# A causal depthwise convolution in two half-rate sums taken by turns, planned transfers, and filler products in TensorE's planned pauses

## The chip, the cores and the metric

One core of a Trainium2 chip runs the whole program. The metric is the time of one execution in device microseconds (us); lower is better. The kernel before took 1378.37 us as the median of three runs (1372.61 to 1379.06). PE is TensorE (products), PEld its weight loads, DVE is VectorE, ACT is ScalarE, POOL is GpSimd, SP is the engine that issues most transfers.

## The reference

One inference step of a two-layer streaming encoder: 512 prompt frames and 64 frames of a running stream, 1024 features. Each layer, cut to what matters:

```
proj = x @ w_in                       # columns q, k, v, conv_a, conv_gate
k, q = rope(k), rope(q)
attn = differential attention, 4 heads (softmax of q k, two maps subtracted, times v)
u    = conv_a * sigmoid(conv_gate)
c    = causal depthwise conv of u, 31 taps, 512 channels, + conv_b
c    = silu(layer_norm(c))
y    = concat(attn, c) @ w_out
x    = layer_norm(alpha * x + y)
x    = layer_norm(alpha * x + relu(x @ w_ff1)^2 @ w_ff2)
```

Outputs are y of both streams and the new k, v and convolution states of both layers.

## The kernel before, in words

All 576 frames are handled at once, features on partitions, in two groups of 288 frames. Products are made in three passes (`tri`, lines 733 to 736): every operand is split into a high and a low part, and high·high, high·low and low·high are summed in one PSUM bank. A layer reads 92 weight units of 128 x 1024 numbers. `weights` (line 830) loads a unit into a `raw` buffer from SP's queue (L861); ScalarE makes the high part `wh` (L891), and the low part `wl` is made in one of two ways: VectorE or GpSimd subtracts (L894), or ScalarE writes minus raw (L875) and a transfer on GpSimd's queue adds the unit from DRAM onto it (L878, "by_dma"); how often the second is used is set by the knob `DM`. Twenty units of layer 1 are split ahead of time during layer 0 (`split_ahead`, L815 and L819).

A layer has five parts: projections with attention and convolution woven into them; the output projection with residuals (L1799, L1804, L1857); a layer norm (`layer_norm`: sums of the residuals L1835, means L1029 and L1034, subtractions L1052, squares L1058 and their adds L1064, variance by products with a column of ones L1006, scale L1133 and L1141, and the split into the next operands L1154); the feed-forward part; and a second layer norm.

The convolution (`conv`, line 1305) is done for each of four tiles of 128 channels over 606 positions (30 of history, 512, 30 of history, 64, with the positions between the streams computed and dropped). Of its 31 taps, the first `NPTS[t]` are products on ScalarE (L1319 with the bias, L1322) that GpSimd adds up (L1325); the others are a chain on VectorE, each a multiply-add into one accumulator in PSUM that waits for the one before it (L1335 and L1337). A closing (L1344, three instructions) adds the two sums and drops the unused positions. Only one tile at a time may hold the VectorE chain (`cv`).

The order of all work is written by a planner in the kernel (`Sched.run`, line 565), before anything runs: every operation is a node with its engines, planned costs (`cV`, `cA`, `cG`, `cP`, `cD`), dependencies, buffers and a priority, and an event loop gives each engine the ready node of the highest priority. A node with several engines goes where it would end first. Priorities and choices come from tables of knobs (`PHASES`), one for each of the eight phases. On the chip every engine keeps its planned order, and waits for what it needs.

Of the kernel before, what the change touches and what calls it, by code (L numbers as in the profile page):

```python
# [16 lines left out]
D = 1024  # L17
# [12 lines left out]
UC = UB - HIST  # L30
S0 = SEQ + HIST
# [54 lines left out]
def cP(n, passes=1):  # L86
# [50 lines left out]
PD = 0.1  # L137
DM, GD, GDL = 0.0, 0.88, 6.5
PRP, PRS = 889.2, -10.4
# [12 lines left out]
PHASES = [{'CH': 4,  # L152
# [3 lines left out]
  'KA': 4,  # L156
  'KB': 8,
  'KR': 4,
  'LD1': 1.46,
  'LD2': 3.53,  # L160
  'LD3': -0.78,
  'LDO': -373.3,
  'LP': 2.08,
  'LPE': 2.98,
  'LPT': 2.46,
  'NPT': '9,9,9,10',
  'PA': 158.2,
# [12 lines left out]
  'QL0': '0 2 4 6',  # L180
  'QL1': '0 2 4 5 6 7',
  'QLF': '0 6 7',
  'RG': 1,
  'RP': [0, 2],
  'RS': 1,
  'S2F': [0, 1, 2, 3, 5],
  'S2H': [0, 2, 4, 7],
  'SHP': 1,
  'SQ': 'k0 q0 g0 a0 v0 g1 a1 q1 g2 a2 k1 v1 g3 a3 q2 k2 v2 q3 k3 v3',
  'VP': 0.39,  # L190
  'VS': 2.22,
# [2237 lines left out]
```

## Time and profile before

| | |
|---|---|
| median of three runs | 1378.37 us |
| profiled execution | 1375.67 us |
| its span, first to last instruction | 1373.9 us |
| TensorE busy | 1308.0 us, 9518 instructions |
| VectorE busy | 1078.1 us, 2206 |
| ScalarE busy | 705.1 us, 1413 |
| GpSimd busy | 302.3 us, 292 |
| mean granted clock of TensorE | 0.977 |
| layer 0: attention, convolution, output projection | about 0 to 276 us |
| layer 0: feed-forward at full pace | 375 to 675 us |
| layer 1: attention, convolution, output projection | about 705 to 950 us |
| layer 1: feed-forward at full pace | 1025 to 1350 us |

Busy time is not pace: products are pipelined, so TensorE counts as busy at half clock too. "PEclk" is the clock that was granted, 1.00 being full. A group's "idle before" is the time that its engine waited ahead of it, with what ended that wait.

### The profile page before, as it was taken

To read this page: it belongs to the slowest core of one execution; us is meant where nothing else is said; L and a number is where in the kernel's file an instruction comes from. 1 tells how busy PE (TensorE), PEld (TensorE's weight loads), DVE (VectorE), ACT (ScalarE), POOL (GpSimd) and SP (SyncE) were. 2 spreads that over 40 slices of the span, in tenths; PEclk is the share of its full clock that TensorE was granted. 3 is DMA by queue.
4 is the path that set the end of the run, shared out by engine and by line. 5 is a ranking of instruction groups with operands and counts; after the bars stand their busy time and mean duration, and the time that the engine had idled before them with its cause. 6 is when DMAs were issued, how large, how long until landed. Compare 5 with 4: busy or idle time off the path is not lost.

```text
span 1373.9 us, 24858 instructions
## 1 busy us (share of the span) xinstructions
PE 1308.0 (95%) x9518; PEld 1264.1 (92%) x9518; DVE 1078.1 (78%) x2206; ACT 705.1 (51%) x1413; POOL 302.3 (22%) x292
## 2 busy tenths in 40 slices
PE   8989989979999999999999999899989999999997
PEld 7878879979899999999998988798889999999996
DVE  5899998777888887878658999868677676767737
ACT  5766677265444444434156657754654443434424
POOL 0456620150000000000144885223400000000013
PEclk9999989989999999999999999899999999999998
DMA  6635533334465645554345444454234343435262
GB/s 220 162 94 140 122 117 106 93 130 156 144 211 165 208 168 192 185 167 139 102 158 204 160 152 121 129 135 118 64 79 117 112 108 108 124 80 144 70 152 69
DMA packets 70102, 186.38 MB, mean 136 GB/s; under 512 B 10848, under 2 KB 16608, under 8 KB 69984
## 3 DMA queue, kind: packets, MB, share of 16 engines
q1 hardware_dynamic: 63504, 161.20, 34.9%
q0 software_dynamic: 6480, 23.60, 10.4%
q8 instruction: 75, 1.23, 0.4%
q14 instruction: 43, 0.35, 0.1%
HBM read 154.11 MB, written 30.65 MB: 134 GB/s over the span
## 4 chain that ended last, share of the span: by engine, by line
PE 72%; DVE 18%; issue 3%; DMA 2%; ACT 2%; POOL 2%; SPq 0%; ACTq 0%; DVEq 0%; POOLq 0%
PE b L734 21%; PE b L735 21%; PE b L736 21%; DVE sc L1337 8%; DMA raw<-in_wu_dram 2%; PE sc L734 1%; PE b L1006 1%; POOL sq L1064 1%; PE sc L736 1%; PE b L1568 1%; PE sc L735 1%; DVE nm L1486 1%; DVE P L1530 1%; DMA wl<-in_wu_dram 1%; PE b L1611 1%
## 5 line engine op out<-in xcount | busy, mean ns | idle before, releaser
L734 PE MATMUL b<-x,wh 128*128 128x288 f32 x1356 | 416.2, 307 | 6.6 <-ACT wh L891 4.0
L736 PE MATMUL b<-x,wl 128*128 128x288 f32 x1356 | 406.1, 299 | 7.0 <-DVE wl L894 4.8
L735 PE MATMUL b<-x,wh 128*128 128x288 f32 x1356 | 406.5, 300 | 1.7 <-DVE x L1215 1.1
L734 PE MATMUL b<-a,wh 128*128 128x288 f32 x1088 | 325.0, 299 | 0.2 <-ACT x L731 0.2
L735 PE MATMUL b<-a,wh 128*128 128x288 f32 x1088 | 321.3, 295 | 0.0
L736 PE MATMUL b<-a,wl 128*128 128x288 f32 x1088 | 321.0, 295 | 0.0
L734 PEld LDWEIGHTS b<-x,wh 128*128 128x128 f32 x1356 | 260.5, 192 | 13.5 <-ACT wh L891 4.0
L736 PEld LDWEIGHTS b<-x,wl 128*128 128x128 f32 x1356 | 260.2, 192 | 8.2 <-DVE wl L894 5.3
L735 PEld LDWEIGHTS b<-x,wh 128*128 128x128 f32 x1356 | 260.6, 192 | 4.0 <-DVE x L1215 2.5
L734 PEld LDWEIGHTS b<-a,wh 128*128 128x128 f32 x1088 | 205.1, 188 | 2.0 <-issue 0.6
L735 PEld LDWEIGHTS b<-a,wh 128*128 128x128 f32 x1088 | 205.4, 189 | 0.5
L736 PEld LDWEIGHTS b<-a,wl 128*128 128x128 f32 x1088 | 205.1, 188 | 0.0
L2273 DVE TENSOR_TENSOR r<-r,b 128x288 f32<-128x288 f32 x192 | 85.7, 450 | 87.6 <-PE b L736 87.3
L1337 DVE SCALAR_TENSOR_TENSOR sc<-ub,par,sc 128x606 f32<-128x606 f32 x160 | 136.2, 851 | 4.2
L878 POOL DMA_DIRECT2D wl<-in_wu_dram x45 | 39.2, 871 | 446.8 <-ACT wl L875 387.6
L1064 POOL TENSOR_TENSOR sq<-sq,sq 128x288 f32<-128x288 f32 x40 | 35.7, 910 | 416.1 <-ACT sq L1058 415.5
L1325 POOL TENSOR_TENSOR r<-r,prod 128x606 f32<-128x606 f32 x72 | 113.7, 1580 | 54.8 <-ACT prod L1322 31.0
L891 ACT CAST wh<-raw 128x1024 fp32r<-128x1024 f32 (+1 forms) x73 | 71.4, 979 | 71.2 <-PE b L735 52.3
L2056 ACT CAST wh<-ckv 128x512 fp32r<-128x512 f32 x104 | 64.1, 620 | 76.7 <-PE b L735 61.2
L894 DVE TENSOR_TENSOR wl<-raw,wh 128x1024 fp32r<-128x1024 f32 (+1 forms) x73 | 84.5, 1161 | 22.3 <-ACT wh L891 21.7
L1884 DVE TENSOR_TENSOR wl<-ckv,wh 128x512 fp32r<-128x512 f32 x104 | 71.1, 685 | 6.0 <-ACT wh L2056 5.8
L875 ACT ACTIVATE wl<-raw 128x1024 fp32r<-128x1024 f32 x45 | 47.7, 1060 | 44.2 <-PE b L736 25.5
(320 smaller groups left out, 2409.9 us busy)
## 6 DMA issues: line engine op xcount, KB each, us to landing
raw<-in_wu_dram SPq DMA_DIRECT2D x110, 512.0 KB, 4.6
wl<-in_wu_dram POOLq DMA_DIRECT2D x45, 512.0 KB, 7.2
wscr<-cs SPq DMA_DIRECT2D x80, 256.0 KB, 2.0
ckv<-in_wu_dram SPq DMA_DIRECT2D x26, 512.0 KB, 3.6
ah<-in_wu_dram SPq DMA_DIRECT2D x26, 512.0 KB, 4.4
cs<-in_wu_dram SPq DMA_DIRECT2D x40, 256.0 KB, 2.8
wh<-wscr SPq DMA_DIRECT2D x20, 512.0 KB, 3.3
wl<-wscr SPq DMA_DIRECT2D x20, 512.0 KB, 4.4
```

The lines of the kernel that those rows point to most:

```text
L734: TE.matmul(o, wh, xh, start=start, stop=False)
L735: TE.matmul(o, wh, xl, start=False, stop=False)
L736: TE.matmul(o, wl, xh, start=False, stop=stop)
L875: S.activation(wt["lo"], wt["raw"], AF.Copy, scale=-1.0)
L891: S.copy(wt["hi"][:, c], wt["raw"][:, c])
L894: e.tensor_tensor(wt["lo"][:, c], wt["raw"][:, c], wt["hi"][:, c].bitcast(F32), op=ALU.subtract)
L1064: e.tensor_tensor(q[a]["t"], q[a]["t"], q[b]["t"], op=ALU.add)
L1325: GP.tensor_tensor(cc[t], cc[t], st[j], op=ALU.add)
L1337: V.scalar_tensor_tensor(st["a0"], win(j), w, st["a0"], op0=ALU.mult, op1=ALU.add)
L1884: e.tensor_tensor(o, a, b, op=ALU.subtract)
L2056: S.copy(tl["wh"][box["i"]][:, off:off + n], src())
L2273: V.tensor_tensor(rr, rr, bk(), op=ALU.add)
```

## The change

**The convolution.** Even and odd frames are taken apart. With e the even and o the odd frames, the 16 even taps and the 15 odd taps make three half-length sums: a = even taps on e, b = odd taps on o (with the bias), c = sums of neighbouring taps on e + o. The even outputs are a + b, the odd ones c − a − b (b one place on), corrected by the bias. b is on ScalarE and GpSimd as before (304 elements, `NPTS` of the 15 taps, what remains on VectorE); a and c are on VectorE, 16 products each of 303 elements, by turns: one of a, one of c. e + o is one addition, on VectorE or GpSimd. The summed taps (`cv`) are made once in a layer. Results lie with the even frames first; the split of the convolution's output into `cmix` puts them back in order (`halves`).

**Fillers.** When the planner's clock stands at a moment at which TensorE has nothing to do, has been busy less than `FT` = 0.6 of the last `FW` = 2 us, and a PSUM bank is free, it plans a product of constants into that bank (`keep`). There are 23 in the program: 12 ahead of the first real product, 8 at the first layer norm of layer 0 and just ahead of it, one at the second, and two at the last.

**Transfers planned.** The accumulating transfer (L878) is planned with a duration on the transfer queue and a latency behind what is queued there (`dm`, `GDL`, `GDS`), not with a fixed 6.5; some other planned costs are changed.

**The tables.** All eight tables of knobs, the split-ahead priorities and `PD` are others. So the whole order of work is another.

What the order of instructions shows for the whole program: accumulating transfers 45 → 60, VectorE's weight subtractions of 1024 elements 65 → 50 (10 → 5 ahead of the first layer norm, 38 → 19 from there to the second layer's start, 2 → 7 in layer 1 up to its first norm), ScalarE's tap products 80 → 112, GpSimd's adds of them 72 → 104, the odd taps on VectorE 0 → 8 (5 and 3). Of layer 0's residual additions of 288 (L1804), all 16 were on VectorE, and 15 are now on GpSimd; of the 12 adds of its sums (L1835), 3 were on GpSimd, and now all are. TensorE's real products are the same.

```diff
+FT, FW, FC = 0.6, 2.0, 0.23
-PD = 0.1
-DM, GD, GDL = 0.0, 0.88, 6.5
+PD = 0.0
+DM, GD, GDL, GDS = 0.0, 0.88, 1.9, 2.93
...
-PHASES = [{'CH': 4,
+PHASES = [{'CH': 3,
...
-  'NPT': '9,9,9,10',
+  'NPT': '15,10,16,15',
...
+    def spare(self, t, busy, avail):
+        if not FT or self.keep is None or busy > t + 1e-9 or not self.free["b"] or not self.left_p():
+            return False
+        return sum(min(b, t) - max(a, t - FW) for a, b in self.recent if b > t - FW) < FT * FW
...
+                        if n.dm:
+                            n.lat = GDL + n.dm + max(0.0, busy["D"] - t - c)
+                            busy["D"] = max(busy["D"], t + c) + n.dm
...
+            if self.spare(t, busy["P"], avail):
+                n = self.op({"P": FC}, lambda e: self.keep(e, self.free["b"][0]))
...
+    def keep(e, k):
+        TE.matmul(tl["b"][k][:, :128], ones_d, ones_d, start=True, stop=True)
+    sch.keep = keep
...
+            V.tensor_tensor(cv[:, :, 1:], taps[:, :, 2::2], taps[:, :, 1::2], op=ALU.add)
+            V.tensor_scalar(cv[:, :, 0], pr[:, P_CB:P_CG], 2.0, None, op0=ALU.mult)
...
-                los.append(op({"G": GD}, acc, (m,), lat=GDL, pri=pri + 1000, two=False))
+                los.append(op({"G": GD}, acc, (m,), lat=GDL + GDS, pri=pri + 1000, two=False))
+                los[-1].dm = GDS
...
         def conv(t, start, outs):
-            hc = UC // 2
-            npt = NPTS[t]
+            npt = min(NPTS[t], W // 2)
...
-                    w = pr[:, cw + j:cw + j + 1]
+                    w = pr[:, cw + 2 * j + 1:cw + 2 * j + 2]
...
-                        st[j] = take("prod")
-                        S.activation(st[j], ub[t][:, j:j + UC], AF.Copy, scale=w)
+                        st[j] = take("prod")[:, :YH + 1]
+                        S.activation(st[j], frames(1, j, YH + 1), AF.Copy, scale=w)
...
+            for j in range(npt, W // 2):
+                def vb(e, j=j):
+                    V.scalar_tensor_tensor(b_(), frames(1, j, YH + 1), pr[:, cw + 2 * j + 1:cw + 2 * j + 2], b_(),
+                                           op0=ALU.mult, op1=ALU.add)
+            def both(e):
+                e.tensor_tensor(cc[t][:, :UH], frames(0, 0, UH), frames(1, 0, UH), op=ALU.add)
...
-            for j in range(npt, W):
+            for j in range(W // 2 + 1):
...
-                        V.scalar_tensor_tensor(st["a0"], win(j), w, st["a0"], op0=ALU.mult, op1=ALU.add)
-                vt = op({"V": cV(UC, True) + 0.06}, va, (*start, pd, vt), acq=("cv", "sc") if j == npt else (), pri=PT)
+                        V.scalar_tensor_tensor(st["a"], frames(0, j, YH), w, st["a"], op0=ALU.mult, op1=ALU.add)
+                def vc(e, j=j):
+                        V.scalar_tensor_tensor(st["c"], cc[t][:, j:j + YH], w, st["c"], op0=ALU.mult, op1=ALU.add)
+                vt = a_end = op({"V": 0.45}, va, (*start, pd, vt), acq=("cv", "sc") if j == 0 else (), pri=PT)
+                vt = op({"V": 0.45}, vc, (sm, vt, ld_n), pri=PT)
...
-                    V.tensor_tensor(a1[:, o:o + n], a1[:, i:i + n], a0[:, b, c:c + n], op=ALU.add)
+                for o, i, n in parts:
+                    V.tensor_tensor(cc[t][:, o:o + n], st["a"][:, i:i + n], b_(n, i), op=ALU.add)
+                for o, i, n in parts:
+                    V.scalar_tensor_tensor(cc[t][:, T // 2 + o:T // 2 + o + n], st["c"][:, i:i + n], cv[:, t, 0:1],
+                                           b_(n, i + 1), op0=ALU.add, op1=ALU.subtract)
+                for o, i, n in parts:
+                    z = cc[t][:, T // 2 + o:T // 2 + o + n]
+                    V.tensor_tensor(z, z, st["a"][:, i:i + n], op=ALU.subtract)
```

More of the change, by code (lines that the diff above doesn't have):

```diff
@@ L407 @@
   'DM': 0.5,
+  'KA': 3,
+  'KB': 0,
+  'KR': 5,
+  'LA': 0.28,
+  'LD1': 1.28,
+  'LD2': -1.07,
+  'LD3': -0.17,
+  'LDO': 100.5,
+  'LDS': 1000,
+  'LP': 0.81,
+  'LPE': 2.12,
+  'LPT': -2.77,
+  'PA': -72.0,
+  'PC': 684.3,
+  'PCN': 1357.5,
+  'PE_': 267.8,
+  'PK': -422.4,
+  'PN': 644.4,
+  'PQ': 9.9,
+  'PR': 562.7,
+  'PS': -860.1,
+  'PT': 1313.0,
+  'PV': 430.4,
+  'PW': -719.8,
+  'PX': -183.1,
+  'QL0': '0 6',
+  'QL1': '0 6 7',
+  'QLF': '0 2 4 6 7',
+  'RG': 0,
+  'RP': [1, 4, 5],
@@ new lines @@
+  'RS': 1,
+  'S2F': [2, 3, 6],
+  'S2H': [1, 3, 4, 5],
+  'SHP': 1,
+  'VP': -0.06,
+  'VS': 1.38,
+  'WP': 0.5,
+  'WP2': -1.19,
+  'WP3': -1.59},
+ {'CH': 3,
+  'CS': 0,
+  'CSTD': 2,
+  'DM': 0.5,
+  'KA': 6,
+  'KB': 8,
+  'KR': 4,
+  'LA': 0.35,
+  'LD1': 0.84,
+  'LD2': 1.43,
+  'LD3': -0.99,
+  'LDO': -1004.4,
+  'LDS': 200,
+  'LP': 0.47,
+  'LPE': 0.86,
+  'LPT': -1.23,
+  'PA': -528.5,
+  'PC': -0.1,
+  'PCN': 1014.7,
+  'PE_': -456.9,
+  'PK': -105.2,
+  'PN': 45.5,
+  'PQ': -41.9,
+  'PR': -328.1,
+  'PS': 427.4,
+  'PT': 1173.3,
+  'PV': 351.8,
+  'PW': -1518.1,
+  'PX': 730.8,
+  'QL0': '0 6 7',
+  'QL1': '0 4 6 7',
+  'QLF': '0 2 4 6 7',
+  'RG': 0,
+  'RP': [0, 1, 2, 3, 4, 6],
+  'RS': 0,
+  'S2F': [3, 5],
+  'S2H': [0, 5, 6, 7],
+  'SHP': 0,
+  'VP': -0.41,
+  'VS': 0.91,
+  'WP': 0.24,
+  'WP2': -0.3,
+  'WP3': -2.36},
@@ new lines @@
+ {'CH': 2,
+  'CSTD': 2,
+  'DM': 0.34,
+  'KA': 1,
+  'KB': 4,
+  'KR': 3,
+  'LA': 0.6,
+  'LD1': 2.87,
+  'LD2': 1.66,
+  'LD3': 1.49,
+  'LDO': 53.6,
+  'LDS': 500,
+  'LP': -1.78,
+  'LPE': -0.59,
+  'LPT': 1.93,
+  'NPT': '14,16,16,13',
+  'PA': 700.3,
+  'PC': -92.8,
+  'PCN': 891.1,
+  'PE_': 839.8,
+  'PK': -847.6,
+  'PN': -840.6,
+  'PR': 113.9,
+  'PS': 194.6,
+  'PT': 497.7,
+  'PV': 529.6,
+  'PW': -141.6,
+  'PX': -1361.9,
+  'QL0': '0 2 4 5 6 7',
+  'QL1': '0 6 7',
+  'QLF': '0 2 4 6',
+  'RG': 0,
+  'RP': [0, 3, 7],
+  'RS': 1,
+  'S2F': [3, 6, 7],
+  'S2H': [0, 1, 2, 3],
+  'SHP': 0,
+  'SQ': 'k0 q0 g0 a0 g1 v0 q1 a1 g2 a2 k1 g3 v1 a3 q2 k2 v2 k3 q3 v3',
+  'VP': 0.43,
+  'VS': 1.36,
+  'WP': -1.48,
+  'WP2': -0.99,
+  'WP3': -1.5},
@@ new lines @@
+ {'CH': 2,
+  'CS': 1,
+  'CSTD': 2,
+  'DM': 0.34,
+  'KA': 2,
+  'KB': 3,
+  'KR': 6,
+  'LA': 0.85,
+  'LD1': 1.91,
+  'LD2': 1.13,
+  'LD3': 2.99,
+  'LDO': 3.4,
+  'LP': 0.42,
+  'LPE': 0.72,
+  'LPT': -0.26,
+  'PA': -314.7,
+  'PC': 196.8,
+  'PCN': 403.2,
+  'PE_': 610.9,
+  'PK': -901.0,
+  'PN': 1022.7,
+  'PQ': -23.5,
+  'PR': 272.9,
+  'PS': -800.1,
+  'PT': 1293.5,
+  'PV': 154.3,
+  'PW': 459.0,
+  'PX': -424.6,
+  'QL0': '0 2 4 6',
+  'QL1': '0 4 6 7',
+  'QLF': '0 4 6 7',
+  'RG': 1,
+  'RP': [1, 2, 6, 7],
+  'RS': 0,
+  'S2F': [0, 6, 7],
+  'S2H': [1, 5],
+  'SHP': 0,
+  'VP': -0.78,
+  'VS': -0.24,
+  'WP': -0.74,
+  'WP2': -0.47,
+  'WP3': 2.29},
@@ L746, in xt, with halves @@
         return take("x")
+    def halves(z):
+        return z.rearrange("p (n two) -> p two n", two=2)
     def at(dt=F32R):
@@ L1207, in x_nodes @@
         ld = chain.pop("x%d%d" % (k, g))
[L1208 removed]
+        d = op({"D": cD(200)}, ld, (xfn.get(k),), acq=("a",) if g == 0 else (), lat=DL, pri=pri)
         sl = GS[g]
```

558 lines of the change are left out of this document (217 added, 341 removed).

## The prediction

> **What bounds the kernel now.** I read the page first, then the table of busy time by stretch, then the chain of work cut to the stretches that fall short, then single lines. The page says that TensorE is the bound over the whole span, with VectorE second:
>
> ```profile
> PE 1308.0 (95%) x9518; PEld 1264.1 (92%) x9518; DVE 1078.1 (78%) x2206; ACT 705.1 (51%) x1413; POOL 302.3 (22%) x292
> ...
> PE   8989989979999999999999999899989999999997
> ...
> PEclk9999989989999999999999999899999999999998
> ```
>
> A mean of 95% hides two kinds of stage. In the table by stretch the columns are the microseconds, then busy time with its instructions for PE, PEld, DVE, ACT and POOL, then the granted clock, the DMA share and GB/s:
>
> ```profile
> 50.00:175.00 125.00, 114.33 (x804) 108.46 (x804) 118.98 (x189) 85.75 (x170) 78.55 (x61) 0.95 0.49 119
> 175.00:225.00 50.00, 46.08 (x313) 39.62 (x312) 44.96 (x111) 40.91 (x102) 9.31 (x8) 0.90 0.33 97
> 276.00:300.00 24.00, 16.47 (x83) 15.06 (x82) 16.48 (x38) 14.45 (x32) 14.59 (x16) 0.72 0.38 131
> 375.00:675.00 300.00, 300.00 (x2264) 299.84 (x2263) 241.90 (x477) 121.76 (x213) 0.00 (x0) 1.00 0.51 170
> 725.00:900.00 175.00, 164.75 (x1166) 151.43 (x1165) 161.29 (x297) 118.62 (x268) 103.33 (x81) 0.96 0.49 150
> 1025.00:1350.00 325.00, 324.94 (x2456) 324.38 (x2454) 225.75 (x469) 137.53 (x238) 18.91 (x22) 1.00 0.41 109
> ```
>
> The two feed-forward stretches (625 us) are full at clock 1.00: nothing planned elsewhere can shorten them. What TensorE can give back lies in the attention and convolution stretches. From 50 to 225 it idles 14.6 us (175 less 114.33 less 46.08) and loses about 10 us to the clock (0.05 of 114 us and 0.10 of 46 us); from 725 to 900 it idles 10.3 us and loses about 6.6; from 276 to 300 it idles 7.5 and loses about 4.6 (0.28 of 16.5 us). In the first and the third VectorE is busy 95% and 92%. The chain of waits, cut to 50–175 and to 725–900, names the work that is waited for; these are its shares by line:
>
> ```profile
> by line: DVE sc L1337 37.0%; issue 6.5%; DMA raw<-in_wu_dram 5.0%; DVE P L1530 4.2%; PE b L734 3.9%; PE b L735 3.5%; PE b L736 3.5%; DVE nm L1486 3.4%; DVE wl L894 2.7%; ACT prod L1322 1.8%; DVE rc L1518 1.8%; ACT wl L875 1.6%; DVE r L1344
> ```
> ```profile
> by line: DVE sc L1337 35.2%; issue 6.9%; PE b L734 4.8%; PE b L1568 4.0%; PE b L735 4.0%; PE b L736 3.9%; DVE P L1530 3.3%; DVE nm L1486 3.1%; DVE nm L1492 2.0%; DVE sc L1335 1.9%; DVE swp L1367 1.9%; PE b L1006 1.7%; PE sc L734 1.7%; DVE r
> ```
>
> L1337 is VectorE's tap of the convolution: 46 us of the chain in the first stretch, 62 in the other. There the softmax pieces that TensorE needs stand in VectorE's queue between taps.
>
> **The change on VectorE.** Lines of VectorE by total time, cut to 50–225 (busy us, mean ns of one, idle before), and below them the taps of 725–900:
>
> ```profile
> L1337 DVE SCALAR_TENSOR_TENSOR sc<-ub,par,sc 128x606 f32<-128x606 f32 x81 | 68.9, 851 | 1.9
> ...
> L894 DVE TENSOR_TENSOR wl<-raw,wh 128x1024 fp32r<-128x1024 f32 x5 | 7.1, 1424 | 0.0
> ...
> L1344 DVE TENSOR_TENSOR r<-r,sc 128x303 f32<-128x303 f32 (+2 forms) x12 | 3.5, 350 | 0.5 <-POOL r L1325 0.5
> ```
> ```profile
> L1337 DVE SCALAR_TENSOR_TENSOR sc<-ub,par,sc 128x606 f32<-128x606 f32 x77 | 65.6, 852 | 2.3
> ```
>
> What a tap of 303 costs no row shows, so I build it. The timeline has six taps in a row, and five subtractions that do not depend on one another; two groups give the slope:
>
> ```profile
> 119.39 5.28 DVE L1337 SCALAR_TENSOR_TENSOR sc<-ub,par,sc 128x606 f32<-128x606 f32 x6
> ```
> ```profile
> 279.91 1.91 DVE L1052 TENSOR_TENSOR r<-r,b 128x288 f32<-128x288 f32 x5
> ```
> ```profile
> L2083 DVE TENSOR_TENSOR ckh<-ah 128x512 f32<-128x512 f32 x26 | 17.8, 685 | 1.8 <-DMA ah<-in_wu_dram 1.8
> ...
> L1052 DVE TENSOR_TENSOR r<-r,b 128x288 f32<-128x288 f32 x56 | 21.7, 447 | 3.3 <-PE b L1034 3.1
> ```
>
> A tap now waits for the one before: (5.28 − 0.85) / 5 = 0.886 us from start to start, 35 ns more than its length. Independent work of 288 elements starts every (1.91 − 0.45) / 4 = 0.365 us, 82 ns less than its length. An element costs (685 − 447) / 224 = 1.06 ns, so a tap of 303 should last 851 − 322 = 530 ns. In turns, neither sum waits for its neighbour: 0.53 − 0.08 = 0.45 us a start. Should each still wait: 0.565 us.
>
> Per layer: before, layer 0 has 87 taps on VectorE (77.1 us at 0.886) and four closings (3.5 us), 80.6 in all; layer 1 has 81 and four, 75.3. After, each has 128 products of the two sums (57.6 us at 0.45), layer 0 five odd taps (2.3) and layer 1 three (1.4), two frame sums (0.8), and four closings of six instructions, three of 256 elements and three of 32. For a closing I take 1.5 us (bounds 1.1, the three long ones at 0.365, and 2.4, all six at 0.4): 6.0. Sum 66.7 and 65.8, so VectorE loses 14 us in layer 0 and 9.5 in layer 1; at 0.565 it would lose nothing (81.4 and 80.5).
>
> The Trainium skill ("VectorE: DVE Perf Modes", section "The DRAIN you can't avoid") says that an instruction of VectorE does not start before the pipe has emptied and that chaining doesn't help, so that the count of instructions should be kept low: it speaks against cutting taps in two. By the page's formula for a two-input fp32 operation, (N+151)/0.96, 303 elements would take 473 ns and the sum an estimated 3 us more per layer. The starts 0.365 us apart above are shorter than that formula's 457 ns for 288, so the trace does not bear it out for independent work.
>
> VectorE, first convolution tile of layer 0; before:
>
> ```order
> L1337 SCALAR_TENSOR_TENSOR sc_119<-ub_544,par_161,sc_119 128x2x303 x3
> L1485 MEMSET sc_118 64x2x64
> L1486 TENSOR_REDUCE nm_594<-sc_118 128x2
> L1337 SCALAR_TENSOR_TENSOR sc_119<-ub_544,par_161,sc_119 128x2x303 x7
> L1485 MEMSET sc_118 64x2x64
> ```
> and now the same place (ub is the even frames, r the frame sums):
> ```order
> L1421 SCALAR_TENSOR_TENSOR sc_118<-r_92,cv_165,sc_118 128x303
> L1414 SCALAR_TENSOR_TENSOR sc_118<-ub_548,par_161,sc_118 128x303
> L1576 MEMSET sc_119 64x2x64
> L1577 TENSOR_REDUCE nm_591<-sc_119 128x2
> L1421 SCALAR_TENSOR_TENSOR sc_118<-r_92,cv_165,sc_118 128x303
> ```
> Whole taps give way to the two sums by turns; softmax work stands between them as before, now behind shorter neighbours.
>
> How much reaches the end: of layer 0's 77 us of taps 46 lie on the chain, so 14 freed give 8. Five weight splits (L894) leave VectorE before the first layer norm, at 1.42 us each by the row above (7.1 us); the chain gives L894 2.7% of 125 us, 3.4 us, of half the splits that remain: I take 2. With about 1 for queueing: −11 in layer 0, at most −24 (the whole shortfall). In layer 1, 62 of 72 us are on the chain: 9.5 freed give 8; but five splits come to VectorE there, up to 7 us, I charge 4: −4.
>
> **What else moves.** ScalarE and GpSimd compute the odd taps, 304 elements instead of 606, 112 products instead of 80 and 104 adds instead of 72. Their rows, and those of the additions of 288 on GpSimd and on VectorE:
>
> ```profile
> L1325 POOL TENSOR_TENSOR r<-r,prod 128x606 f32<-128x606 f32 x72 | 113.7, 1580 | 54.8 <-ACT prod L1322 31.0 <-issue 20.8
> ...
> L1322 ACT ACTIVATE prod<-ub,par 128x606 f32<-128x606 f32 x72 | 56.7, 801 | 11.9 <-POOL r L1325 11.5
> ...
> L1064 POOL TENSOR_TENSOR sq<-sq,sq 128x288 f32<-128x288 f32 x40 | 35.7, 910 | 416.1 <-ACT sq L1058 415.5
> ...
> L1835 DVE TENSOR_TENSOR sg<-sg,r 128x288 f32<-128x288 f32 x34 | 16.1, 473 | 1.0
> ...
> L1804 DVE TENSOR_TENSOR r<-r,x 128x288 f32<-128x288 f32 x32 | 15.6, 491 | 0.9
> ```
>
> At about 0.95 us an addition takes 104 × 0.95 = 99 us of GpSimd instead of 114, and stays behind VectorE: nothing. Fifteen more weights get their low half by an accumulating transfer from GpSimd's queue, 17 more of them in the first feed-forward stretch, where TensorE is full: nothing. But in layer 0, 15 residual additions and 9 more of the sums' 12 ahead of the first layer norm go to GpSimd. GpSimd there, before:
>
> ```order
> L878 DMA wl_90<-in_wu_dram 128x1024
> L1064 TENSOR_TENSOR sq_102<-sq_102,sq_103 128x288
> L1064 TENSOR_TENSOR sq_104<-sq_104,sq_105 128x288
> L1064 TENSOR_TENSOR sq_106<-sq_106,sq_103 128x288
> L1064 TENSOR_TENSOR sq_102<-sq_102,sq_104 128x288
> L1064 TENSOR_TENSOR sq_102<-sq_102,sq_106 128x288
> L1835 TENSOR_TENSOR sg_108<-sg_108,r_98 128x288
> ```
> and now (sg is the sum that the mean's product reads):
> ```order
> L1896 TENSOR_TENSOR r_94<-r_94,x_2504 128x288
> L1927 TENSOR_TENSOR sg_107<-r_97,r_91 128x288
> L1927 TENSOR_TENSOR sg_107<-sg_107,r_95 128x288
> L1927 TENSOR_TENSOR sg_107<-sg_107,r_92 128x288
> L1927 TENSOR_TENSOR sg_107<-sg_107,r_96 128x288
> L1927 TENSOR_TENSOR sg_107<-sg_107,r_93 128x288
> L1927 TENSOR_TENSOR sg_107<-sg_107,r_98 128x288
> ```
> The sum is now six GpSimd links in a row, before each half's mean. TensorE's planned pause at the same place, before and now:
> ```order
> L1034 MATMUL b_115<-r_91,ones_d 128x288
> L734 MATMUL b_117<-x_2987,wh_83 128x288
> L735 MATMUL b_117<-x_2988,wh_83 128x288
> L736 MATMUL b_117<-x_2987,wl_87 128x288
> L734 MATMUL b_117<-x_3001,wh_83 128x288
> ```
> ```order
> L782 MATMUL b_116<-x_3189,wh_84 128x288
> L783 MATMUL b_116<-x_3188,wl_88 128x288
> L786 MATMUL b_114<-ones_d 128x128 x6
> L781 MATMUL b_114<-x_3130,wh_85 128x288
> L782 MATMUL b_114<-x_3131,wh_85 128x288
> ```
> Six filler products now stand where TensorE will wait for the normalised x. They can be weighed with the stall of today:
>
> ```profile
> 276.00:284.00 8.00, 2.73 (x16) 2.05 (x14) 7.98 (x21) 7.91 (x20) 6.48 (x9) 0.95 0.17 65
> 284.00:297.00 13.00, 10.75 (x46) 10.13 (x47) 6.24 (x13) 4.83 (x9) 7.51 (x7) 0.50 0.57 187
> ```
> ```profile
> 284.97 0.61 PE L736 MATMUL b<-x,wl 128*128 128x288 f32 x1 [4.83 <-DVE wl L894]
> ```
> ```profile
> L1539 PE MATMUL b<-ident,P 128*128 128x128 f32 x80 | 15.9, 300 | 7.2 <-DVE P L1530 4.3 <-DVE rc L1517 1.9 <-DVE ob L1615 0.6
> ```
>
> After 5 us of pause the clock is half for 13 us, with 10.75 busy: 5.4 us lost. The nearest row prices a filler at 0.30 us, so 23 cost 7 us if all stood on the path, and they stand in pauses. The Trainium skill ("TensorE: Matmul & The Clock Gate", Part 1) says that the clock halves after an idle window of some 3.4 us and returns after a busy one; the row at 0.50 behind the pause agrees. Gain: up to 5.4 from the clock and 4.83 from the split, which now stands ahead of the norm's subtractions; loss: 9 sums at 0.91 instead of 0.47, 4.0, and half of the 15 residuals at 0.42 more, 3. I take 0, bounds −10 and +10. Twelve fillers stand before the first real product:
>
> ```profile
> 0.00:4.00 4.00, 0.00 (x0) 0.00 (x0) 0.46 (x1) 2.12 (x3) 0.86 (x12) 1.00 0.47 123
> 4.00:10.00 6.00, 5.97 (x19) 4.87 (x20) 4.27 (x10) 4.12 (x11) 0.00 (x0) 1.00 0.87 269
> ```
>
> The first 19 products run 0.31 us apart, though they follow each other at 300/2264 = 0.133 us in the full stretch. Fillers started at 1 us at half pace (0.6 each) end near 8: they delay the start by 4 and spare up to 3.4. Zero, give or take 2.
>
> **Sum.** −11 − 4 + 0 + 0 = −15 us against the profiled execution (1375.67 us, span 1373.9), which is 2.7 under the median: 1378.4 − 15 = 1363 us.
>
> **Rivals.** (A) *Both attention stretches become bound by TensorE*: all 24 us of the first shortfall and half of the second's 17 go, and 5 of the norm: −37, 1341. For it speaks the chain; against it, that softmax, rotary and split work stay on VectorE. (B) *The halves don't pay*: each tap waits as today, 0.565 us, and conv work is equal; left are the splits, 0 to −5: 1376. Against it: nothing between neighbours depends. The Trainium skill's section on the drain, quoted above, would have it come out near this. (C) *Slower: GpSimd's sums at layer 0's norm.* They decide when GpSimd needs over about 1 us an addition, as in its row at 282.07 below; the 24 additions moved there at 1.2 instead of 0.48 end 17 us later, and the pause behind brings a half clock (5): −15 + 17 + 5 = +7, 1385.
>
> ```profile
> 282.07 7.19 POOL L1064 TENSOR_TENSOR sq<-sq,sq 128x288 f32<-128x288 f32 x6 [0.46 <-ACT sq L1058]
> ```
>
> (D) *No difference to see*: with every instruction moved, gains are given back at places I cannot see; within 7 us of 1378.
>
> **How the numbers follow.** This kernel's measurement tells about 0.5% (6.9 us) from no change. Forecast (−8 to −28): 0.50; A: 0.12; B and D: 0.20; C: 0.18. Faster 0.62, same 0.20, slower 0.18. The forecast's own range is 1350 to 1370; A below and B, D and part of C above widen it to 1342–1384, which leaves out about a tenth on either side.
>
> **What would show it.** Right: taps of 303 starting 0.45 us apart; VectorE's busy time about 25 us lower before the first norm; TensorE's idle and half clock between 50 and 225 down from 24 us to about 13; feed-forward stretches of 300 and 325 us as now; no clock of 0.50 at the first norm. Wrong: taps 0.565 apart (B), TensorE waiting on sg from GpSimd for over 5 us (C), or waits on wl transfers in the feed-forward stretches.

## The result: 1387.8 us, one per cent slower

The changed kernel takes 1387.79 us (median of 7 runs, 1384.36 to 1397.49), the kernel before 1375.06 beside it (7 runs, 1372.61 to 1379.06): ratio 1.0102, 95% interval 1.0069 to 1.0135. The forecast was 1363. Ratios below are to the kernel before on the same chip; 0.01 of ratio is 13.7 us, and gains are differences of such ratios.

The changed kernel's page, the rows that were shown of before:

```profile
PE 1317.8 (95%) x9594; PEld 1273.3 (92%) x9594; DVE 1079.7 (78%) x2345; ACT 693.6 (50%) x1396; POOL 300.6 (22%) x365
...
PE   9989999988999999999999989898989999999996
...
PEclk9989999999999999999999999999999999999998
```

Up to the last subtraction of layer 0's first norm VectorE is busy 235.6 us, for 242.1 before: 6 us less, where the forecast had about 25 less before that norm. The same stretches as before, in the table by stretch:

```profile
50.00:175.00 125.00, 114.26 (x786) 107.15 (x785) 117.84 (x242) 89.28 (x187) 61.08 (x76) 0.95 0.55 133
175.00:225.00 50.00, 46.55 (x351) 41.97 (x351) 45.58 (x107) 38.85 (x94) 14.52 (x13) 1.00 0.59 167
276.00:300.00 24.00, 19.81 (x131) 18.19 (x131) 19.46 (x37) 16.46 (x36) 16.75 (x21) 0.93 0.48 147
375.00:675.00 300.00, 295.55 (x2207) 292.91 (x2206) 220.20 (x453) 130.77 (x224) 12.08 (x14) 1.00 0.64 193
725.00:900.00 175.00, 161.95 (x1150) 151.46 (x1149) 160.05 (x348) 108.69 (x256) 73.59 (x84) 0.96 0.43 139
1025.00:1350.00 325.00, 322.72 (x2432) 322.11 (x2430) 238.82 (x500) 117.03 (x188) 15.24 (x18) 1.00 0.38 104
```

From 50 to 225 TensorE idles 14.2 us, before 14.6: no gain but in the clock. From 276 to 300 it is better (clock 0.93 for 0.72, 119 products besides 12 of fillers, for 83). The first feed-forward stretch, full before, now lacks 57 of 2264 products, with a DMA share of 0.64 for 0.51. Where the time goes shows best in the moment at which the n-th product of the first pass (`tri`'s first line, 2936 products in each trace) starts, counted in both:

| n of 2936 | place | before | after | difference |
|---|---|---|---|---|
| 490 | end of layer 0's attention part | 273.8 | 271.1 | −2.7 |
| 711 | start of its feed-forward | 384.9 | 379.3 | −5.6 |
| 1442 | end of its feed-forward | 676.4 | 679.1 | +2.7 |
| 1881 | end of layer 1's attention part | 914.4 | 912.5 | −1.8 |
| 1995 | behind its first norm | 973.9 | 982.3 | +8.4 |
| 2900 | end | 1339.6 | 1349.6 | +10.1 |

So the way to layer 0's feed-forward part gains 5.6 us, not 11; that feed-forward part loses 8; and layer 1's first norm loses 10. In layer 1's attention part the count gains 4.5 us, as forecast, but the two orders run these products at different times within a part. By a second measure there is no gain: from the last subtraction of layer 0's second norm to the first mean of layer 1's first norm (L1029, now L1090) it takes 242.4 us before and 243.9 after. The norm's loss shows in both: from that mean to the end of its last scaling (L1133, now L1194) it takes 36.3 us before and 45.9 after. In the attention parts, the timeline of VectorE has the taps like this (start, length):

```profile
106.33 0.54 DVE L1421 SCALAR_TENSOR_TENSOR sc<-r,cv,sc 128x303 f32<-128x303 f32 x1
106.90 0.54 DVE L1414 SCALAR_TENSOR_TENSOR sc<-ub,par,sc 128x303 f32<-128x303 f32 x1
107.48 0.54 DVE L1421 SCALAR_TENSOR_TENSOR sc<-r,cv,sc 128x303 f32<-128x303 f32 x1
108.05 0.54 DVE L1414 SCALAR_TENSOR_TENSOR sc<-ub,par,sc 128x303 f32<-128x303 f32 x1
```

They start 0.572 us apart (mean of 168 pairs of neighbours in the trace, 0.55 to 0.58): a tap's length and 35 ns, as in a chain. The two sums are independent, but each tap acts as if it waited for the tap right before it, which belongs to the other sum. Both sums lie in one tile (`sc`, halves 0 and 1); whether that is the cause is tested below. Where something else follows a tap, it starts after 0.45 us in the median.

In the first feed-forward part, the chain of waits from 425 to 680 us was TensorE's products but for 2%; first before, then after:

```profile
by line: PE b L736 32.7%; PE b L735 32.6%; PE b L734 32.5%; POOL sq L1064 1.0%; DVE r L1052 0.6%; PE b L1034 0.2%; PE b L1029 0.2%; ACT sq L1058 0.2%; DVE r L2300 0.1%; issue 0.0%
```
```profile
by line: DMA wscr<-cs 20.3%; DMA cs<-in_wu_dram 18.8%; PE b L783 11.7%; PE b L781 11.7%; PE b L782 11.6%; DMA ah<-in_wu_dram 5.0%; DVE cs L879 3.7%; ACT cs L875 3.2%; issue 3.2%; DVE wl L1976 2.8%; DVE r L2365 1.6%; DMA ckv<-in_wu_dram 1.6%
```

`cs` is the one buffer of the split-ahead loop (load, ScalarE's cast L875, VectorE's subtraction, two stores). ScalarE's waits there (us in total, times, longest), and how long the `raw` loads of weights took from issue to landing between 375 and 675, first before, then after:

```profile
ACT cs L815 <- DMA cs<-in_wu_dram: 22.0, 13, 3.7
```
```profile
raw<-in_wu_dram SPq DMA_DIRECT2D x28, 512.0 KB, 4.0
```
```profile
ACT cs L875 <- DMA cs<-in_wu_dram: 66.7, 23, 5.8
```
```profile
raw<-in_wu_dram SPq DMA_DIRECT2D x27, 512.0 KB, 7.0
...
wl<-in_wu_dram POOLq DMA_DIRECT2D x14, 512.0 KB, 7.6
```

Fourteen accumulating transfers run in this window, from GpSimd's queue, where none did; `raw` and `cs` come by SP's. ScalarE stands in its order at a split-ahead load that is not there, and the weights behind it come late. In layer 1's first norm the chain from 945 to 985 goes through one such transfer (start, length):

```profile
957.43 1.06 ACT wl L935
958.78 9.61 DMA wl<-in_wu_dram
```

### The profile page after: what moved, and what is told of

Its sections match the earlier page's. It is cut to its first block, busy times and chain, and to the rows that moved or that the text cites. A ratio compares the mean times of both kernels' runs of the same rounds, so it can differ in the third digit from the quotient of the medians.

```text
span 1386.0 us, 25348 instructions
## 1 busy us (share of the span) xinstructions
PE 1317.8 (95%) x9594; PEld 1273.3 (92%) x9594; DVE 1079.7 (78%) x2345; ACT 693.6 (50%) x1396; POOL 300.6 (22%) x365
## 4 chain that ended last, share of the span: by engine, by line
PE 53%; DVE 22%; DMA 12%; ACT 4%; issue 3%; POOL 0%; DVEq 0%; ACTq 0%; SPq 0%; POOLq 0%
PE b L781 15%; PE b L783 15%; PE b L782 15%; DMA wscr<-cs 4%; DMA cs<-in_wu_dram 4%; DVE sc L1414 3%; DVE sc L1421 3%; PE b L1067 1%; DMA wl<-in_wu_dram 1%; DVE cs L879 1%; DVE nm L1577 1%; PE sc L781 1%; DMA ah<-in_wu_dram 1%; DVE P L1621 1%; PE sc L783 1%
## 5 line engine op out<-in xcount | busy, mean ns | idle before, releaser
L938 POOL DMA_DIRECT2D wl<-in_wu_dram x60 | 52.4, 874 | 772.9 <-ACT wl L935 398.9
L2148 ACT CAST wh<-ckv 128x512 fp32r<-128x512 f32 x104 | 63.7, 618 | 66.7 <-PE b L782 50.8
L952 ACT CAST wh<-raw 128x1024 fp32r<-128x1024 f32 (+1 forms) x58 | 55.7, 960 | 70.6 <-PE b L782 50.9
L1392 POOL TENSOR_TENSOR r<-r,prod 128x304 f32<-128x304 f32 x104 | 79.1, 761 | 47.3 <-ACT prod L1389 22.3
L935 ACT ACTIVATE wl<-raw 128x1024 fp32r<-128x1024 f32 x60 | 63.5, 1058 | 39.9 <-PE b L783 34.7
L955 DVE TENSOR_TENSOR wl<-raw,wh 128x1024 fp32r<-128x1024 f32 (+1 forms) x58 | 65.6, 1133 | 18.3 <-ACT wh L952 17.7
L879 DVE TENSOR_TENSOR cs<-cs 128x512 fp32r<-128x512 f32 x40 | 30.8, 771 | 47.4 <-ACT cs L875 47.2
L1421 DVE SCALAR_TENSOR_TENSOR sc<-r,cv,sc 128x303 f32<-128x303 f32 x120 | 64.4, 537 | 3.3
```

Source lines behind the costliest of these rows:

```text
L935: S.activation(wt["lo"], wt["raw"], AF.Copy, scale=-1.0)
L938: GP.dma_start(wt["lo"], wu[l, i], accum_op=ALU.add)
L952: S.copy(wt["hi"][:, c], wt["raw"][:, c])
L955: e.tensor_tensor(wt["lo"][:, c], wt["raw"][:, c], wt["hi"][:, c].bitcast(F32), op=ALU.subtract)
L1392: GP.tensor_tensor(b_(), b_(), st[j], op=ALU.add)
L1421: V.scalar_tensor_tensor(st["c"], cc[t][:, j:j + YH], w, st["c"], op0=ALU.mult, op1=ALU.add)
```

## The experiments

Two theories: the taps wait for each other since they share a tile, which eats the forecast gain; and accumulating transfers are late in places where the forecast gave them no price. Rivals: the engine drains behind every tap whatever the tile, the split-ahead priority, the fillers, the new tables as a whole.

### The taps

**own_tile.** The c sum goes into SBUF, the order is the same:

```diff
-st["a"], st["c"] = st["s"][:, 0, :YH], st["s"][:, 1, :YH]
+st["a"], st["c"] = st["s"][:, 0, :YH], csum_t
```

> The changed kernel with one thing different: the sum of neighbouring taps (c) lies in a tile of its own in SBUF, and no longer in the second half of the tile that holds the sum of even taps (a). The order of the instructions is the same on every engine; only the wait of each tap changes, from the tap right before it to the one before that. Theory 'one tile, one wait' (the two sums wait for each other because waits are set by tile): taps of 303 elements start about 0.45 us apart instead of 0.573, VectorE is busy with other work 15 us earlier in each attention part, and the time falls by 4 to 12 us, to 1376 to 1384. Rival 'the engine drains behind every multiply-add': the taps stay 0.573 us apart and the time stays at 1388 within 3 us. Third: the taps come closer, but the attention parts are bound elsewhere: 0.45 us apart, and no change of time above 3 us.

1391.43 us, ratio 1.0103 (1.0075 to 1.0131): no gain. But the taps moved. VectorE and GpSimd in its timeline:

```profile
107.00 0.55 DVE L1421 SCALAR_TENSOR_TENSOR csum_t<-r,cv,csum_t 128x303 f32<-128x303 f32 x1
107.18 1.67 POOL L1462 TENSOR_TENSOR r<-r,cs 128x576 f32<-128x576 f32 x1
...
107.47 0.53 DVE L1414 SCALAR_TENSOR_TENSOR sc<-ub,par,sc 128x303 f32<-128x303 f32 x1
107.92 1.26 DVE L1421 SCALAR_TENSOR_TENSOR csum_t<-r,cv,csum_t 128x303 f32<-128x303 f32 x1
...
109.10 0.53 DVE L1414 SCALAR_TENSOR_TENSOR sc<-ub,par,sc 128x303 f32<-128x303 f32 x1
```

Where no tap is held, starts are 0.45 to 0.47 us apart in these rows (0.443 in the median of the trace), so the engine does not drain behind each tap. But the c tap at 107.92, both of whose inputs now lie in SBUF, stands until GpSimd's operation ends at 108.85; the a taps, with one input in PSUM, never do (none of 120 took over 0.54 us). The Trainium skill ("SBUF — State Buffer", "SBUF: two separate sides") says that a VectorE instruction with two SBUF inputs and a GpSimd instruction that reads SBUF lock each other out of a shared port pair for a whole instruction; the rows agree. The c taps' mean rose from 537 to 669 ns. The 33 that took over 0.62 us, all begun during a GpSimd operation, cost 16 us more than at 0.53 us each, most of the 22 us that 168 starts could gain at 0.131 us each (0.572 less 0.441, the start in split_sc below):

```profile
L1421 DVE SCALAR_TENSOR_TENSOR csum_t<-r,cv,csum_t 128x303 f32<-128x303 f32 x120 | 80.3, 669 | 0.2
L1414 DVE SCALAR_TENSOR_TENSOR sc<-ub,par,sc 128x303 f32<-128x303 f32 x120 | 63.2, 527 | 0.1
```

**own_bank.** c in a PSUM bank of its own, taken from the four b banks, so that the order changes too:

```diff
-st["c"] = st["s"][:, 1, :YH]
+st["c"] = take("b")[:, :YH]
...
-acq=("cv", "sc") if j == 0 else ()
+acq=("cv", "sc", "b") if j == 0 else ()
```

> The changed kernel with the sum of neighbouring taps (c) in a PSUM bank of its own (one of the four b banks, taken with the a sum and given back with it); the half of the sc tile that it lay in stays unused. The planner has one bank less during a convolution, and so writes another order. In the run with c in SBUF the taps came 0.455 us apart where GpSimd was silent, but single c taps took 1.24 us while GpSimd added. Theory 'one tile, one wait, and PSUM keeps out of GpSimd's way': all taps about 0.455 us apart, none of 1.2 us, mean of a c tap 0.53 to 0.55 us; VectorE has 15 us less to wait in each attention part, and the time falls by 4 to 14 us, to 1374 to 1384. Rival 'the attention parts are bound elsewhere' (TensorE, 91 % busy from 50 to 175, or the order): taps at 0.455, time 1388 within 4 us.

1386.92 us, 1.0106 (1.0072 to 1.014). Neighbouring taps start 0.44 us apart, none held up. At product 600 it is 10 us ahead of the kernel before; at the start of the feed-forward part it loses 14 (TensorE runs 400 instructions in 300 to 375 us, 499 in the changed kernel). The planner had a bank less and wrote another order, so this run could not decide.

**fewer_taps.** Three of sixteen taps of each sum are left out, and every other instruction stays in its place. In both taps:

```diff
+if j in (3, 8, 13):
+    return
```

> The changed kernel with three of the sixteen taps left out of each sum (24 of 128 taps a layer; the convolution is not whole), every other instruction in the same order. The 128 taps of a layer then take what they would at 0.466 us each, near the 0.45 that was forecast, without any move of other work: 24 x 0.573 = 13.8 us of VectorE less in each layer. Theory 'the false wait costs what the forecast wanted from the convolution': the time falls by 8 to 15 us, to 1373 to 1380, about 10 of it in layer 0. Rival 'VectorE's taps do not bound the attention parts': 1388 within 4 us.

1365.72 us, 0.9945 (0.9921 to 0.997): 21.6 us less for 27.5 us of taps: more than expected. Most of what VectorE saves on taps comes off the time, so the taps bound the attention parts.

**split_sc.** All the work done, in the same order, each `sc` buffer made of two tiles in the same PSUM banks:

```diff
-tl["sc"] = [ps_p.tile([128, 2, 512], F32, ...) for i in range(CAPS["sc"])]
+tl["sc"] = [Two([ps_p.tile([128, 512], F32, ...) for j in range(2)]) for i in range(CAPS["sc"])]
...
-V.tensor_reduce(s["nm"], s["sc"][:, :, :nk], ...)
+[V.tensor_reduce(s["nm"][:, a:a + 1], s["sc"][:, a, :nk], ...) for a in range(2)]
```

> The changed kernel, whole, in the same order, with each buffer of two PSUM banks (sc) made of two tiles, so that the two sums lie in different tiles and still in PSUM. The softmax's maximum and mask over both banks become two instructions each: 40 more reductions at about 0.16 us of fixed cost (1.228 us for 1024 elements and 0.425 for 256 give 0.157 + 1.05 per 1024) and 32 more memsets of about 0.1, so 9.6 us more of VectorE; 256 taps at 0.455 for 0.573 are 30 less. With 27.5 us of taps left out the time fell by 21.6. Theory 'one tile, one wait': taps 0.455 us apart, none of 1.2 us, and the time falls by 10 to 18 us, to 1370 to 1378. Rival 'something else than the tap's wait makes the attention parts late': 1388 within 4 us.

1354.01 us, 0.9854 (0.9796 to 0.9911): 34 us less than changed, more than expected. Its timeline, and its stretch from 50 to 175:

```profile
107.27 0.52 DVE L1417 SCALAR_TENSOR_TENSOR sc<-ub,par,sc 128x303 f32<-128x303 f32 x1
107.72 0.52 DVE L1424 SCALAR_TENSOR_TENSOR sc<-r,cv,sc 128x303 f32<-128x303 f32 x1
108.16 0.52 DVE L1417 SCALAR_TENSOR_TENSOR sc<-ub,par,sc 128x303 f32<-128x303 f32 x1
108.59 0.52 DVE L1424 SCALAR_TENSOR_TENSOR sc<-r,cv,sc 128x303 f32<-128x303 f32 x1
```
```profile
50.00:175.00 125.00, 122.27 (x893) 115.37 (x892) 120.08 (x295) 97.48 (x210) 66.44 (x79) 0.99 0.62 151
```

Starts are 0.441 us apart. For the taps only the cut into tiles has changed, so the taps' wait was the program's, and neither the engine's drain nor the banks made it. From 50 to 175 TensorE runs 893 instructions where it ran 786, at a clock of 0.99. Of the 34 us, some 21 come in the attention and convolution parts with their norms (15 in layer 0, 6 in layer 1, by the count of products); the 168 waits that are gone were 22 us. Another 12 come where the feed-forward parts begin (7 and 5 us): there TensorE puts products into one half of an `sc` buffer while VectorE reads the other, and waited. TensorE's idle time from 300 to 375 us fell from 6.2 us to 0.9. The longest of its waits there, from 300 to 390 us, in the kernel before and the changed one, are 2.9 of the 6.2; with two tiles they are gone:

```profile
PE sc L734 <- DVE r L2271: 3.6, 6, 0.6
```
```profile
PE sc L781 <- DVE r L2363: 2.9, 5, 0.6
```

**split_pad and b_split.** How much of the 34 us is the taps, and would the mend have helped the kernel before? split_pad adds to split_sc an instruction after each pair of taps; b_split gives the kernel before the two tiles, and each of its taps becomes two:

```diff
+V.tensor_scalar(pad_t[:, :136], frames(0, 0, 136), 1.0, None, op0=ALU.mult)
```
```diff
-V.scalar_tensor_tensor(st["a0"], win(j), w, st["a0"], op0=ALU.mult, op1=ALU.add)
+[V.scalar_tensor_tensor(st["a0"][:, h, :hc], win(j)[:, h, :], w, st["a0"][:, h, :hc],
+                        op0=ALU.mult, op1=ALU.add) for h in range(2)]
```

> The run with each sc buffer as two tiles, and after each pair of taps one more instruction on VectorE (a product of 136 elements into a tile that nobody reads), sized so that a pair takes about 2 x 0.455 + 0.236 = 1.146 us, as with the false wait; all else as in that run. Theory 'the taps are most of it': 15 us of VectorE come back in each layer, and the time goes up from 1354 to 1372 to 1384. Rival 'other false waits on the sc halves are most of it': 1354 to 1365.

> The kernel before with each sc buffer as two tiles: its taps of 606 elements become two of 303 in different tiles (2 x 0.455 = 0.910 for 0.886 us, 2 us more of VectorE a layer), and the maximum and mask of the softmax two instructions each (9.6 us more in all). Theory 'the mend helps the new convolution above all': 1366 to 1378, so that the new convolution with its mend is 12 to 24 us ahead of the old one with the same mend. Rival 'the mend helps both alike': 1350 to 1360.

split_pad: 1397.43 us, 1.0151 (1.0107 to 1.0196), 41 us more than split_sc and above what either theory expected. The pads were dearer than planned:

```profile
L1425 DVE TENSOR_SCALAR pad_t<-ub 128x136 f32<-128x136 f32 x128 | 54.3, 425 | 0.2
```

They read and write SBUF; the 44 that took over 0.25 us (0.81 in the mean) all overlap a GpSimd instruction, and the other 84 took 0.22. From the end of the tap ahead to the end of the pad they cost 44 us in all: so a microsecond of VectorE in these parts is worth nearly one of the whole. b_split: 1373.93 us, 0.9982 (0.996 to 1.0004): no gain. It too wins 4 to 6 us at the start of each feed-forward part, but loses 5 and 7 in the attention parts and their norms; why there was not tried. So with the same mend the new convolution is 18 us ahead of the old one (ratio 0.9854 against 0.9982).

**true_cost.** The taps planned at what they take:

```diff
-vt = a_end = op({"V": 0.45}, va, ...
+vt = a_end = op({"V": 0.575}, va, ...
-vt = op({"V": 0.45}, vc, (sm, vt, ld_n), pri=PT)
+vt = op({"V": 0.575}, vc, (sm, vt, ld_n), pri=PT)
```

> The changed kernel with the taps of both sums planned at 0.575 us, what they take on the chip, and not at 0.45. Theory 'the wait is what costs': the taps still start 0.573 us apart, and the time stays at 1388 within 5 us. Rival 'the order is wrong, since it was drawn with taps too cheap': the time falls by 5 to 10 us, with shorter waits of TensorE in the attention parts.

1397.83 us, 1.0177 (1.0147 to 1.0206): 10 us slower, outside what either theory expected. The taps still start 0.57 us apart; a truer price with the same tables gave another order, and a worse one.

### The transfers

**ffn_dm0, prp_before, no_acc_23.** No accumulating transfers planned in phases 2 and 3; the split-ahead priorities of before; and the changed order with the 19 transfers of phases 2 and 3 left out:

```diff
-  'DM': 0.5,
+  'DM': 0,
```
```diff
-PRP, PRS = 1741.8, -10.7
+PRP, PRS = 889.2, -10.4
```
```diff
-GP.dma_start(wt["lo"], wu[l, i], accum_op=ALU.add)
+phi in (2, 3) or GP.dma_start(wt["lo"], wu[l, i], accum_op=ALU.add)
```

> The changed kernel with the knob DM at 0 in the feed-forward part of layer 0 and the layer norm behind it (phases 2 and 3), as it was before: 19 accumulating transfers less, and 19 subtractions of 1024 elements more on VectorE or GpSimd. Theory 'late transfers' (the accumulating transfers crowd the queues while the split-ahead loads run, ScalarE stands in order at a late split-ahead load and TensorE starves): the first feed-forward part is back at the pace of before, TensorE 300 of 300 us from 375 to 675, and the time falls by 7 to 10 us, to 1378 to 1381. Rival 'split-ahead priority' or 'another place': no change above 3 us.

> The changed kernel with the split-ahead priorities of before (889.2 and -10.4 for 1741.8 and -10.7), all else as changed. Theory 'late transfers': split-ahead loads still meet the accumulating transfers, so no gain above 3 us (1385 to 1391). Rival 'split-ahead priority' (the load runs too early, ahead of the weights that are needed sooner): the feed-forward part of layer 0 is back at 300 us of TensorE in 375 to 675, and the time falls by 7 to 10 us.

> The changed kernel with the 19 accumulating transfers planned in phases 2 and 3 (first feed-forward part and the layer norm behind it) left out, so that these low parts are minus raw; every other instruction in the same order, and nothing takes the transfers' place. Theory 'late transfers': without them TensorE is busy 299 to 300 of 300 us from 375 to 675 and the time falls by 6 to 10 us, to 1378 to 1382, as it did where the planner put subtractions in their place (1382.7). Rival 'the split-ahead loads are late for themselves': under 3 us.

1382.66 us (1.0054, 1.003 to 1.0078), 1391.89 (1.0115, 1.0083 to 1.0148) and 1382.25 (1.0045, 1.0025 to 1.0064). Without the transfers the feed-forward part is full again, with nothing in their place (7.8 us gained), or nearly so, with subtractions in their place (6.6 us; TensorE busy 298.73 of 300). With the priorities of before it stays at 297.09 and nothing is gained, so the priority is not it. The stretch, and ScalarE's wait from 425 to 680 us, in no_acc_23:

```profile
375.00:675.00 300.00, 299.94 (x2265) 299.38 (x2264) 227.65 (x467) 133.56 (x228) 4.24 (x5) 1.00 0.51 170
```
```profile
ACT cs L875 <- DMA cs<-in_wu_dram: 20.2, 13, 2.9
```

```profile
raw<-in_wu_dram SPq DMA_DIRECT2D x26, 512.0 KB, 4.1
```

66.7 us of waiting are 20.2 again, and the raw loads land after 4.1 us in place of 7.0.

**no_acc, no_acc_fewer_taps, b_no_acc.** All accumulating transfers left out: 60 in the changed kernel, the same with fewer taps, and 45 in the kernel before:

```diff
-GP.dma_start(wt["lo"], wu[l, i], accum_op=ALU.add)
+True or GP.dma_start(wt["lo"], wu[l, i], accum_op=ALU.add)
```

> The changed kernel with all 60 accumulating transfers left out (low parts of these units are minus raw), every other instruction in the same order. Theory 'late transfers in more places than one': beside the 6 to 10 us of the first feed-forward part, the first layer norm of layer 1 comes back by 4 to 8 us (a transfer of 9.3 us was on the chain there), so 1370 to 1378. Rival 'only the first feed-forward part': as the run with 19 left out, within 3 us.

> Both at once: three of sixteen taps of each sum and all 60 accumulating transfers left out, the order of the rest as changed. Theory 'two costs in different places': the two gains add up, 18 to 30 us below the changed kernel, 1358 to 1370, which is what the forecast of 1363 supposed. Rival 'they hide each other': no more than the larger of the two.

> The kernel before with its 45 accumulating transfers left out (these low parts are minus raw), the order of the rest as it was. Theory 'the change made them late' (15 more, 19 in the first feed-forward part where before had none): the kernel before gains under 7 us, 1367 to 1375. Rival 'they cost both kernels alike': it gains 15 to 20 us, 1354 to 1360, and the change's share of the 21 us is little.

1367.71 us (0.995, 0.9928 to 0.9973), 1351.49 (0.9821, 0.9785 to 0.9857) and 1361.98 (0.9907, 0.9877 to 0.9937). The transfers cost the changed kernel 20.9 us and the kernel before 12.8, between what the two theories expected; what the change made worse is 8 us, the feed-forward part's 7.8. By the count of products up to the first feed-forward part both gain alike without them, 7.6 and 9.1 us. Both costs together give 38.6 us, nearly their sum (42.5): they are in different places. In no_acc the chain of layer 1's first norm has no transfer in it, and the norm is 3 us shorter (42.8 us from first mean to last scaling, for 45.9), still 6.5 longer than before.

**dm_235.** ffn_dm0 with phase 5 as well, for that norm:

```diff
-  'DM': 0.34,
+  'DM': 0,
```

> As the run with no accumulating transfers in phases 2 and 3 (1382.66 us), and none in phase 5 either (output projection and first layer norm of layer 1, DM 0.34 to 0). In that run the chain from 955 to 965 us goes through ScalarE's minus raw and one accumulating transfer of 9.3 us, with TensorE granted 0.80 to 0.85 from 960 to 980 us where it had 1.00 before. Theory 'late transfers, in this layer norm too': the norm is back, 3 to 8 us faster, 1375 to 1380. Rival 'the norm is late for another reason' (its sums, its splits): 1382 within 3 us, the clock still 0.80 to 0.85 there.

1391.34 us, 1.013 (1.01 to 1.0159): a miss, 10 us slower than ffn_dm0. The edit did not take the transfer away; another unit's stood in the same place:

```profile
961.30 8.81 DMA wl<-in_wu_dram
971.34 3.24 PE sc L1067 x24
```

The 10 us were lost ahead of the norm: by the count of products it falls from level with ffn_dm0 at product 1800 to 13 us behind it at product 1881.

**split_acc_true.** split_sc with the transfer's latency planned at 7.43 us:

```diff
-DM, GD, GDL, GDS = 0.0, 0.88, 1.9, 2.93
+DM, GD, GDL, GDS = 0.0, 0.88, 4.5, 2.93
```

> The two banks as tiles of their own, and the accumulating transfer planned with a latency of 7.43 us behind what is queued (GDL 4.5 + GDS 2.93) and not 4.83; the 60 of them landed after 7.2 us in the mean. The planner writes another order. Theory 'planned too cheap': products that need these low parts are put later, the first feed-forward part comes back, and the time is 5 to 10 us below that of the two banks alone. Rival 'their number' (they crowd the split-ahead loads whatever the plan): the same as the two banks alone within 4 us.

1373.16 us, 0.9993 (0.9972 to 1.0014): 19 us slower than split_sc. As with true_cost, a truer price with the same tables wrote a worse order, and neither theory foresaw it.

### The rest

**no_fill**, and **tables_before** with the tables and split-ahead priorities of before (`NPT` as changed):

```diff
-FT, FW, FC = 0.6, 2.0, 0.23
+FT, FW, FC = 0, 2.0, 0.23
```
```diff
-PHASES = [{'CH': 3,
+PHASES = [{'CH': 4,
...
-PRP, PRS = 1741.8, -10.7
+PRP, PRS = 889.2, -10.4
```

> The changed kernel without fillers (FT at 0): none of the 23 products of constants. The forecast on record put the 12 at the start at nothing within 2 us. Theory 'nothing': 1388 within 3 us. Rival 'the fillers stand in the way of the first products': 2 to 3 us faster, 1385. Other rival 'they hold the clock up': slower by 3 to 6 us, with half clock in 5 to 15 us and at the first layer norm.

> The changed code (new convolution, fillers, transfers planned) with the eight tables and the split-ahead priorities of before; only the numbers of odd taps on ScalarE (NPT) stay as changed, since those of before count another kind of tap. Theory 'the new tables bring the late transfers, and the convolution is worth nothing with its taps at 0.573 us' (32 taps of 0.573 are 18.3 us a tile, 22 of 0.886 were 19.5): 1375 within 6 us, the first feed-forward part at 300 us of TensorE in 375 to 675. Rival 'the new convolution itself costs the time' (its ScalarE products and GpSimd adds): 1383 to 1395, with the loss in the attention parts and the layer norm behind them.

1393.47 us (1.0111, 1.0048 to 1.0174): the fillers are worth nothing that shows, in a run too uneven to tell 3 us. 1385.68 (1.0079, 1.0052 to 1.0106): the old tables bring the feed-forward part back (300.00 of 300 us) but not the time. The expected 1375 did not come; the time is in the range of its rival, the new convolution itself. By the count of products the loss lies in layer 1, from 7 us ahead at product 1442 to 7 behind at product 1995. The taps still wait here (0.572 us), which is the likely cause, but this run doesn't part them from the convolution's other work. So the new tables bring the feed-forward part's loss, but not the whole.

**split_ffn_dm0**, split_sc and ffn_dm0 together:

> The same with the two banks as tiles of their own and no accumulating transfers in phases 2 and 3 (the run of 1382.66 us with this mend). Theory 'two costs in different places': 1364 to 1373, faster than before, and the nearest to the forecast of 1363 with all work done. Rival 'only one of them can be had': 1374 to 1383.

1348.54 us, 0.9807 (0.9777 to 0.9838): faster than both kernels, by 26 and 41 us, with all work done, and better than either theory expected.

## Why the prediction was wrong

- **The taps** ("In turns, neither sum waits for its neighbour: 0.53 − 0.08 = 0.45 us a start"). This step failed. The length was right (0.537 us against 0.53), and so was the start of independent taps: 0.441 us once they were independent. But in the changed kernel they were not: each waited, 0.572 us. The prediction read independence from the arithmetic and not from what each tap waits for, though its own order rows show both sums as one `sc`. With its 0.565 us the sum of VectorE's work was right to give no gain from the convolution; the 5.6 us up to the feed-forward part are no more than the 7.1 of the five splits that left VectorE there.
- **Rival B** had the right condition, at a chance it shared with D (0.20), for the wrong reason. Its price, 1376, lacked the other steps. The Trainium skill ("VectorE: DVE Perf Modes", "The DRAIN you can't avoid") reports that a semaphore after each instruction cost eight copies nothing extra; here a wait for the tap right before costs 0.131 us (0.572 against 0.441), and taps that wait only for the last tap of their own sum start before the tap ahead of them has ended (after 0.441 us of its 0.529).
- **What a tap is worth.** The 8 us a layer for freed taps were low for layer 0 and about right for layer 1: the mend gave 15 and 6 there, and 21.6 us came from 27.5 us of taps left out.
- **The transfers** ("in the first feed-forward stretch, where TensorE is full: nothing"). This step failed: it cost 8 us. A full TensorE was taken as cover, but it is full only while weights come in time: beside the 14 transfers the `raw` loads, though on another queue, landed after 7.0 us in place of 4.0. The prediction named "waits on wl transfers in the feed-forward stretches" as a sign of being wrong; the waits that came were on the loads beside them.
- **Layer 1's first norm**: no term at all. It lost 10 us. Without accumulating transfers (no_acc) it is 3 us shorter; the other 6 to 7 stay open. With the old tables it takes 41.8 us, so part of it may be the new order.
- **First norm of layer 0 and fillers** (0, bounds 10; 0, give or take 2): within their bounds. The count of products gains 3 us from the end of layer 0's attention part to its feed-forward part. The fillers delay the first real product from 4.0 to 6.1 us, but the twentieth starts at 16.9 us for 17.1. Rival C's time, 1385, came near the measured one by luck; its mechanism did not come: GpSimd's adds of 304 took 0.76 us (0.95 was estimated) and its sums of 288 took 0.80, under the point of 1 us:

```profile
L1392 POOL TENSOR_TENSOR r<-r,prod 128x304 f32<-128x304 f32 x104 | 79.1, 761 | 47.3 <-ACT prod L1389 22.3 <-issue 20.4
...
L1927 POOL TENSOR_TENSOR sg<-sg,r 128x288 f32<-128x288 f32 x17 | 13.7, 804 | 8.7 <-DVE r L2392 6.9 <-DVE r L1949 1.3
```

With the taps' wait mended, the forecast's mechanism is there: 1354 us, below its 1363. That it is below is luck in part: 12 us of the mend's 34, at the starts of the feed-forward parts, were no term of the forecast.

## What to carry to other kernels

Two chains by turns help only if the program lets them overlap: look at what each instruction waits for, not only at the data, and put independent sums into separate tiles. A stage at 100% is no cover for more transfers: its loads' landing times are the slack. A truer price in a planner is not by itself a better order: with the tables of knobs left as they were, truer prices cost 10 and 19 us here.

## What was not expected of the hardware

A multiply-add with both inputs in SBUF stood still until a running GpSimd operation had ended (1.26 us in place of 0.55), one with its sum in PSUM never did. Accumulating transfers of 512 KB landed 7.2 us after their issue in the median, and plain loads beside them 7.0 in place of 4.0. Maxima over both halves (256 to 1024 elements), cut in two, cost little: the 80 half reductions kept VectorE busy 38.8 us in split_sc, the 40 whole ones 36.2 in the changed kernel.
